# A decoder layer with streamed weights: another order of the mixer's column blocks, and order edges for its two recurrences

## The chip, the cores and the metric

The kernel runs on one core of a Trainium2 chip. A core has a matrix engine (TensorE, PE in the profile), a vector engine (VectorE, DVE), a scalar engine (ScalarE, ACT), GpSimd (POOL), a queue engine (SyncE, SP) and 16 DMA engines. Each engine executes its own list of instructions in order, and semaphores make one engine wait for another. The metric is the device time of one execution in microseconds; less is better.

## The reference

One layer for 256 tokens of width 2048, in float32: a half-step SwiGLU feed-forward part (width 5632), a mixer, and a second half-step feed-forward part, each followed by a layer norm. The mixer puts two kinds of heads side by side: differential attention (8 heads) and RWKV-7 (16 heads of size 64, a recurrence over the tokens).

```python
x = layer_norm(alpha * x + 0.5 * swiglu(x, ffn1_w_gate[l], ffn1_w_up[l], ffn1_w_down[l]),
               ln1_g[l], ln1_b[l])
p = x @ w_in[l]
o_attn = diff_attn_group(p[..., :ATTN_COLS], lambda_q1[l], lambda_k1[l],
                         lambda_q2[l], lambda_k2[l], attn_norm_g[l], lambda_init)
o_rwkv = rwkv7_group(p[..., ATTN_COLS:], rwkv_mu[l], rwkv_w0[l], rwkv_w2[l],
                     rwkv_a0[l], rwkv_a2[l], rwkv_g2[l], rwkv_k_k[l], rwkv_k_a[l],
                     rwkv_r_k[l], rwkv_gn_g[l], rwkv_gn_b[l])
mix = jnp.concatenate([o_attn, o_rwkv], axis=-1) @ w_out[l]
x = layer_norm(alpha * x + mix, ln2_g[l], ln2_b[l])
x = layer_norm(alpha * x + 0.5 * swiglu(x, ffn2_w_gate[l], ffn2_w_up[l], ffn2_w_down[l]),
               ln3_g[l], ln3_b[l])
```

The heart of the RWKV-7 part is a state that every token updates:

```python
sa = jnp.einsum('bhvk,bhk->bhv', state, -kk_t)
state = (state * w_t[:, :, None, :]
         + sa[..., None] * (kk_t * a_t)[:, :, None, :]
         + v_t[..., None] * k_t[:, :, None, :])
return state, jnp.einsum('bhvk,bhk->bhv', state, r_t)
```

## The kernel before

**Streaming.** The 256 tokens are two tiles of 128 (tt = 0 and 1). All weights pass through the core once, in blocks of 256 x 512. `Stream.block` loads such a block as `raw` on SP's DMA queue (3 buffers). ACT rounds it to the matrix engine's 32-bit format as `wh` (L128), and DVE forms the rest as `wl` (L129); each has 7 buffers. PE then makes three products for each 128 rows of a block (L105 to L107: high part by `wh`, high part by `wl`, low part by `wh`), into an accumulator `acc` of 128 x 512. These are the stream matmuls: six for a block and token tile. Tile 1 follows tile 0 four blocks later (`LAG`). The high and low parts of the activations, `xh` and `xl`, are made by ACT (L78) and DVE (L79).

**The mixer** works on four groups: r1 and r2 are the two halves of the RWKV heads, a1 and a2 those of the attention heads. Each group needs three column blocks of `w_in` (512 columns, eight stream steps each): r, k and v for RWKV, q, k and v for attention. A finished accumulator is copied to `tm` (L338) and transposed (L342). The rest of a group's work is written as Python generators: `rwkv_group` prepares the recurrence, runs it and makes r's output (L683 to L727), `rwkv_values` prepares the values, and `attn_heads` computes two heads each. After every stream step `run_bg` advances the generators in turn (`bg`), until the costs that they yield have used up a budget of 1.6 (`BG`). So the text of the program interleaves the generators with the stream, and a scheduler with a timeline then fixes the list of every engine.

**The recurrence of a group** goes over four chunks of 64 tokens. Before it, a triangular inverse is computed by DVE (L577 and L579, 31 pairs), written to memory as `dY` and `dYT`, and read back in another layout as `TT` and `YT` (L583 to L595, all issued by ACT). Products with them on PE follow (L602, L613), then transposes (L623). In each chunk PE's L636 goes to DVE's copy L638, PE's L644 to the copies L645 (DVE) and L646 (ACT), PE's L652 to the new state on DVE (L657 to L662), and L669 and L675 make the output. r1 must be past its chain before r2 may use its buffers (`until`).

**After the recurrence** comes what this document calls r's tail: means on PE (L689), their subtraction on DVE (L690), squares on ACT (L693), sums on PE (L699), logarithm and exponential on ACT, each with its table load (L700, L702), four steps on DVE (L704, L707, L709 and, with PE's L720 and L723, the gate at L724), and the split into `xh` and `xl`.

**w_out** is applied in three parts of its rows, numbered 0 = a1, 1 = a2, 2 = r1, 3 = r2: first (0, 2), then (1,), then (3,). Before each part `ready` drains the groups that it needs. A part adds its product into `y` (L866), and behind the last one the statistics (L868) and `ln_tail` (L176 to L185, and transposes L72) make LN2, on which the second feed-forward part waits.

The column blocks come in the order r1: k r v; a1: v k q; r2: k r v; then a1 is drained; a2: v k q.

## Time and profile before

| | us |
|---|---|
| median of 3 runs (2021.23 to 2022.83) | 2022.36 |
| the profiled execution's own time | 2021.85 |
| span of the profiled execution | 2020.1 |
| mean clock granted to PE | 0.989 of full |

The mixer's recurrences and w_out lie between about 760 and 1290 us of the span; the feed-forward parts are on both sides. A row of the page gives line, engine, operation, tiles (out<-in), count, busy time, the mean of one in ns, and the idle time before with what ended it. A row of a timeline gives start, duration, engine, line, operation and tiles, and in brackets the idle time ahead of it with what ended that. In the rows of windows the numbers in brackets are instruction counts.

### The profile page before, as it was taken

How to read it: one execution, taken by the hardware profiler on the slowest of the kernel's cores; microseconds unless marked ns; L12 is line 12 of the kernel's file. 1: busy time of each engine (PE TensorE's matmuls, PEld its weight loads, DVE VectorE, ACT ScalarE, POOL GpSimd, SP SyncE). 2: the span in 40 equal slices, each digit the busy share in tenths (PEclk: the TensorE clock that was granted, in tenths of full speed). 3: DMA queues.
4: the chain of work that ended last, by engine and by line, in shares of the span. 5: the costliest groups of instructions: out<-in, count | busy, mean ns of one | idle time of the engine just before them, and what ended most of it. 6: DMA issues, size and time to landing. Idle time of an engine off the chain costs nothing. (4 is left out here: it accounts for less than half of the span.)

```text
span 2020.1 us, 24928 instructions
## 1 busy us (share of the span) xinstructions
PE 1976.9 (98%) x9671; PEld 1614.6 (80%) x9671; DVE 1149.0 (57%) x1420; ACT 887.6 (44%) x1100; POOL 33.9 (2%) x68
## 2 busy tenths in 40 slices
PE   9999999999999999999999988999999999999997
PEld 7888888888888878888777777788888888888886
DVE  5555544445554566776677866755554444555455
ACT  5444433344444337645574444444443334444432
POOL 0200000000000000000000000000000000000000
PEclk9999999999999999999999979999999999999999
DMA  7766666667666556556435624666666666766553
GB/s 248 214 188 195 186 190 202 205 192 229 193 187 189 188 171 194 177 160 178 139 86 177 198 84 148 210 198 188 196 185 190 203 204 191 230 193 187 189 188 125
DMA packets 202008, 373.35 MB, mean 185 GB/s; under 512 B 22826, under 2 KB 24944, under 8 KB 201120
## 3 DMA queue, kind: packets, MB, share of 16 engines
q1 hardware_dynamic: 182928, 350.53, 58.0%
q10 hardware_dynamic: 17440, 14.29, 2.4%
q0 software_dynamic: 1520, 6.93, 1.0%
q8 instruction: 76, 1.25, 0.3%
q14 instruction: 44, 0.36, 0.1%
HBM read 364.10 MB, written 7.60 MB: 184 GB/s over the span
## 5 line engine op out<-in xcount | busy, mean ns | idle before, releaser
L129 DVE TENSOR_TENSOR wl<-raw,wh 128x1024 fp32r<-128x1024 f32 (+1 forms) x665 | 808.2, 1216 | 662.4 <-ACT wh L128 661.3
L128 ACT CAST wh<-raw 128x1024 fp32r<-128x1024 f32 (+1 forms) x665 | 695.2, 1046 | 851.9 <-PE acc L107 736.8
L107 PE MATMUL acc<-wh,xl 128*128 128x512 f32 (+1 forms) x1952 | 740.7, 391 | 1.6 <-DVE xl L79 1.6
L106 PE MATMUL acc<-wl,xh 128*128 128x512 f32 (+1 forms) x1952 | 736.7, 392 | 1.0 <-DVE wl L129 1.0
L105 PE MATMUL acc<-wh,xh 128*128 128x512 f32 (+1 forms) x1952 | 725.5, 392 | 9.0 <-ACT xh L78 7.6
L105 PEld LDWEIGHTS acc<-wh,xh 128*128 128x128 f32 x1952 | 367.9, 189 | 88.7 <-ACT xh L78 9.3
L106 PEld LDWEIGHTS acc<-wl,xh 128*128 128x128 f32 x1952 | 368.1, 189 | 77.5 <-issue 2.0
L107 PEld LDWEIGHTS acc<-wh,xl 128*128 128x128 f32 x1952 | 367.8, 188 | 76.3 <-DVE xl L79 2.0
L107 PE MATMUL acc<-wh,hh 128*128 128x512 f32 x704 | 258.0, 395 | 0.0
L106 PE MATMUL acc<-wl,hh 128*128 128x512 f32 x704 | 256.7, 394 | 0.0
L105 PE MATMUL acc<-wh,hh 128*128 128x512 f32 x704 | 256.0, 394 | 0.0
L106 PEld LDWEIGHTS acc<-wl,hh 128*128 128x128 f32 x704 | 132.0, 187 | 31.4
L107 PEld LDWEIGHTS acc<-wh,hh 128*128 128x128 f32 x704 | 132.0, 188 | 31.2
L105 PEld LDWEIGHTS acc<-wh,hh 128*128 128x128 f32 x704 | 132.0, 188 | 30.9
L230 DVE TENSOR_TENSOR hh<-tr,hh 128x512 fp32r<-128x512 f32 x44 | 30.4, 691 | 64.4 <-ACT hh L229 64.4
L229 ACT CAST hh<-tr 128x512 fp32r<-128x512 f32 x44 | 25.8, 586 | 91.7 <-PE tr L221 91.6
L218 DVE SCALAR_TENSOR_TENSOR h<-sg,acc 128x512 f32<-128x512 f32 x44 | 30.3, 688 | 35.6 <-PE acc L107 35.6
L213 ACT ACTIVATE sg<-acc 128x512 f32<-128x512 f32 x44 | 26.4, 600 | 43.8 <-PE acc L107 43.7
L577 DVE TENSOR_TENSOR itmp<-U,Y 64x31 f32<-64x31 f32 (+15 forms) x62 | 20.6, 332 | 11.5 <-DMA U<-dU 10.2
L221 PEld LDWEIGHTS tr<-ident,h 128*128 128x128 f32 x176 | 21.8, 139 | 5.7
L221 PE MATMUL tr<-ident,h 128*128 128x128 f32 x176 | 26.3, 272 | 0.0
L579 DVE TENSOR_TENSOR Y<-Y,itmp 64x31 f32<-64x31 f32 (+15 forms) x62 | 20.6, 332 | 1.4
(247 smaller groups left out, 750.2 us busy)
## 6 DMA issues: line engine op xcount, KB each, us to landing
raw<-in_ffn_w_up_dram SPq DMA_DIRECT2D x176, 512.0 KB, 3.9
raw<-in_ffn_w_down_dram SPq DMA_DIRECT2D x176, 512.0 KB, 4.1
raw<-in_ffn_w_gate_dram SPq DMA_DIRECT2D x175, 512.0 KB, 3.9
raw<-in_w_in_dram SPq DMA_DIRECT2D x96, 512.0 KB, 3.9
raw<-in_w_out_dram SPq DMA_DIRECT2D x32, 512.0 KB, 4.6
rc<-xs ACTq DMA_DIRECT2D x16, 256.0 KB, 4.0
lng<-in_ln_g_dram POOLq DMA_DIRECT2D x3, 1024.0 KB, 7.0
lnb<-in_ln_b_dram POOLq DMA_DIRECT2D x3, 1024.0 KB, 9.3
```

Of the source, the lines that this page charges most:

```text
L105: T.matmul(a, hi, wh[:, j, :w], start=(ki + j == 0), stop=False)
L106: T.matmul(a, hi, wl[:, j, :w], start=False, stop=False)
L107: T.matmul(a, lo, wh[:, j, :w], start=False, stop=(ki + j == last))
L128: SC.copy(out=wh[:, c, :w], in_=raw[:, c, :w])
L129: V.tensor_tensor(out=wl[:, c, :w], in0=raw[:, c, :w], in1=wh[:, c, :w].bitcast(F32), op=ALU.subtract)
L213: SC.activation(out=s, in_=acc, func=AF.Silu)
L218: V.scalar_tensor_tensor(out=h, in0=sg[tt], scalar=0.5, in1=acc, op0=ALU.mult, op1=ALU.mult)
L221: T.transpose(tr[:, i, :], h[:, i * P:(i + 1) * P], ident)
L229: SC.copy(out=hi, in_=tr)
L230: V.tensor_tensor(out=lo, in0=tr, in1=hi.bitcast(F32), op=ALU.subtract)
L577: V.tensor_tensor(out=tv, in0=U[:, 0:j, j:j + 1].to_broadcast([64, j, 32 - j]), in1=Y[:, j:j + 1, j:32].to_broadcast([64, j, 32 - j]), op= ...
L579: V.tensor_tensor(out=Y[:, 0:j, j:32], in0=Y[:, 0:j, j:32], in1=tv, op=ALU.add)
```

## The change

Six things are edited together; the change adds and removes no arithmetic.

- The column blocks come in the order r1: k r v; a1: v, k; r2: k, r; a1: q; r2: v; a2: q; then a1 is drained; a2: v, k. `rwkv_cols` and `attn_cols` take one block per call, and r2's recurrence has its inputs one block sooner.
- w_out's parts come in the order (0, 2), (3,), (1,): r2's is second, a2's last.
- The recurrences' generators go to a list of their own, `hot`. `run_bg` gives it the budget first, and the attention generators another (1.0, `AT`, if `hot` moved).
- `mark` and `behind` add order edges: the last matmul of a recurrence step is marked, and the first matmul of tile 0, two stream steps later, must come behind it in PE's list. The edge orders the list and adds no semaphore.
- The yields' costs change (0.6 to 4.0 ahead of the inverse, 1.0 to 1.6 in it, 0.6 to 6.0 behind its DMAs, 0.6 to 0.8 in the chain).
- Two of the four `y` tiles are put where r2's `TT` and `YT` were.

In the changed kernel the lines are numbered otherwise. L105, L106 and L107 are L118, L121 and L122; L128 is L143; L78 is L79; L338 and L342 are L367 and L371; L583, L584, L591 and L595 are L617, L618, L625 and L629; L602 is L636; L636, L644, L652, L669 and L675 are L671, L680, L689, L707 and L713; L689, L699, L720 and L723 are L727, L737, L758 and L761; L766 is L806, L821 is L861.

```diff
+AT = 1.0
...
+            self.hot = []
             self.bg = []
-            self.credit = 0.0
+            self.credit = [0.0, 0.0]
             self.hooks = {}
             self.step = 0
+            self.marks = []
+
+        def mark(self, inst):
+
+            self.marks.append((self.step, inst.ins))
+
+        def behind(self, inst):
+            while self.marks and self.marks[0][0] + 2 <= self.step:
+                first = self.marks.pop(0)[1]
+                tc.add_manual_dep(inst.ins, first.name, mybir.DependencyInfo(mybir.DependencyClass.NoSync, mybir.DependencyReason.DATA),
+                                  reason="issue order")
...
-                T.matmul(a, hi, wh[:, j, :w], start=(ki + j == 0), stop=False)
+                m = T.matmul(a, hi, wh[:, j, :w], start=(ki + j == 0), stop=False)
+                if tt == 0 and j == 0:
+                    self.behind(m)
...
+        def run_bg(self, budget):
+            moved = False
+            for i, lst in enumerate((self.hot, self.bg)):
+                self.credit[i] = min(self.credit[i], 0.0) + (AT if moved else budget)
+                while self.credit[i] > 0:
+                    cost = self.advance(lst)
+                    if cost is None:
+                        break
+                    moved = True
+                    self.credit[i] -= cost
...
+        def rwkv_state(g, prev=None):
+            st = {"prev": prev, "g": g}
             if prev is not None:
                 prev["next"] = st
             st["gen"] = rwkv_group(g, st)
-            stream.bg.append(st["gen"])
+            stream.hot.append(st["gen"])
+            return st
...
+            i = "rkv".index(name)
+            stream.block(w_in, R0 + i * AW + g * NB, NB, KX, x_lhs, lambda tt, acc: done(tt, acc, i), budget=BG)
...
-            yield 0.6
+            yield 4.0
...
-                    yield 1.0
+                    yield 1.6
...
-            yield 0.6
+            yield 6.0
...
+            order = stream.mark
             for c in range(4):
                 ps = bank("sm", (P, 4, 64))
                 for p in range(4):
                     for e in range(2):
                         k = halves[1 - e] if c == 0 else slice(0, P)
-                        T.matmul(ps[halves[e], p, :], Q[k, p, c, e, 0:64], SV[k, p, c, e, :], start=True, stop=True)
+                        m = T.matmul(ps[halves[e], p, :], Q[k, p, c, e, 0:64], SV[k, p, c, e, :], start=True, stop=True)
                 Rs = mp.tile([P, 4, 64], F32, tag="Rs", name=nm("Rs"))
                 V.tensor_copy(out=Rs, in_=ps)
-                yield 0.6
+                order(m)
+                yield 0.8
...
+                if st["cols"] == 6:
                     st["left"] = 2
                     st["gens"] = [attn_heads(g, st, (i, i + 2)) for i in range(2)]
                     stream.bg.extend(st["gens"])
...
-        r1 = rwkv_cols(0)
-        a1 = attn_cols(0)
-        r2 = rwkv_cols(1, r1)
+        r1, a1, a2 = rwkv_state(0), attn_group(0), attn_group(1)
+        for name in "krv":
+            rwkv_cols(r1, name)
+        attn_cols(a1, "v")
+        attn_cols(a1, "k")
+        r2 = rwkv_state(1, r1)
+        rwkv_cols(r2, "k")
+        rwkv_cols(r2, "r")
+        attn_cols(a1, "q")
+        rwkv_cols(r2, "v")
+        attn_cols(a2, "q")
         stream.drain(gens(a1))
-        a2 = attn_cols(1)
+        attn_cols(a2, "v")
+        attn_cols(a2, "k")
         stream.flush()
...
-        parts = [(0, 2), (1,), (3,)]
+        parts = [(0, 2), (3,), (1,)]
...
                 yt = [hp.tile([P, 2, NB], F32, tag="H3", name=nm("yt")), qq[:, 0].rearrange("p a s -> p (a s)").rearrange("p (t n) -> p t n", t=2),
-                      hp.tile([P, 2, NB], F32, tag=HT["k"], name=nm("yt"))]
-                yj = hp.tile([P, 2, NB], F32, tag="H5", name=nm("yv"))
-                yv = [yj[:, t] for t in range(2)]
-                y = [[yt[n][:, t, :] for n in range(3)] + [yv[t]] for t in range(2)]
+                      hp.tile([P, 2, NB], F32, tag=HT["lw"], name=nm("yt")), hp.tile([P, 2, NB], F32, tag=HT["T1"], name=nm("yt"))]
+                y = [[yt[n][:, t, :] for n in range(4)] for t in range(2)]
```

The first place is PE's list where w_out's first part (0, 2) ends. In the list of the change, `acc_9546` is an accumulator of part (0, 2), the `sm` tiles are r2's tail, `at_9656` and `at_9684` are transposes of a2's last outputs, and `acc_9702` is the first accumulator of the next part, (3,):

```order
L727 MATMUL sm_9459<-BKc,bones 128x256 x2
L727 MATMUL sm_9463<-BKc,bones 128x256 x2
L861 MATMUL at_9656<-ident,ot_9562 128x128 x2
L861 MATMUL at_9684<-ident,ot_9608 128x128
L737 MATMUL sm_9512<-Q,bones 128x256 x2
L737 MATMUL sm_9516<-Q,bones 128x256 x2
L758 MATMUL sm_9592<-gs_5688,Q 128x256 x2
L761 MATMUL sm_9592<-gs_5689,Q 128x256 x2
L861 MATMUL at_9684<-ident,ot_9608 128x128
L758 MATMUL sm_9598<-gs_5688,Q 128x256 x2
L761 MATMUL sm_9598<-gs_5689,Q 128x256 x2
L118 MATMUL acc_9702<-wh_9697,xh_9688 128x512
```

In the list before, the same stretch has r2's recurrence (`sm_8863` to `sm_8943`) and a2's transposes between the end of part (0, 2) and the first matmul of part (1,), which is `acc_9702` there:

```order
L636 MATMUL sm_8863<-SV_8235,Q 64x64 x8
L821 MATMUL at_9576<-ident,ot_9496 128x128 x2
L644 MATMUL sm_8874<-Rs_8872,TT_8541 64x64 x8
L652 MATMUL sm_8885<-SV_8235,BT_8641 64x64
L669 MATMUL sm_8925<-Q,SV_8235 64x64
L652 MATMUL sm_8885<-SV_8235,BT_8641 64x64 x3
L652 MATMUL sm_8885<-SV_8235,BT_8642 64x64 x4
L669 MATMUL sm_8925<-Q,SV_8235 64x64 x7
L675 MATMUL sm_8925<-AR,St_8822 64x64 x8
L821 MATMUL at_9580<-ident,ot_9528 128x128 x2
L636 MATMUL sm_8943<-SV_8235,Q 64x64 x8
L105 MATMUL acc_9702<-wh_9697,xh_9688 128x512
```

r2's tail comes later before, between the stream matmuls of part (1,) (`acc_9822`) and the first of part (3,), `acc_9870`:

```order
L699 MATMUL sm_9031<-Q,bones 128x256 x2
L699 MATMUL sm_9035<-Q,bones 128x256 x2
L720 MATMUL sm_9091<-gs_5688,Q 128x256 x2
L723 MATMUL sm_9091<-gs_5689,Q 128x256 x2
L106 MATMUL acc_9822<-wl_9838,xh_9688 128x512
L107 MATMUL acc_9822<-wh_9837,xl_9689 128x512
L105 MATMUL acc_9822<-wh_9837,xh_9688 128x512
L106 MATMUL acc_9822<-wl_9838,xh_9688 128x512
L107 MATMUL acc_9822<-wh_9837,xl_9689 128x512
L720 MATMUL sm_9167<-gs_5688,Q 128x256 x2
L723 MATMUL sm_9167<-gs_5689,Q 128x256 x2
L105 MATMUL acc_9870<-wh_9865,xh_9856 128x512
```

So r2's recurrence has moved from behind part (0, 2) to among its matmuls, and r2's tail has moved to where the recurrence was, with no stream matmul in it.

The second place is ACT's list around r2's inverse (`dY`). In the list of the change, `tm_8743` and `tm_8781` are copies of a2's k, and `xh_8795` and `xh_8799` are the halves of a1's output that part (0, 2) begins with:

```order
L367 COPY tm_8743<-acc_8562 128x512
L617 DMA dY_8040<-Y_8048 64x1024
L618 DMA dYT_8041<-U_8046 32x1024
L79 CAST xh_8807<-og_7655 128x512
L143 CAST wh_9078<-raw_9077 128x1024
L143 CAST wh_9147<-raw_9146 128x1024
L783 COPY qq<-tr_8443 128x4x128
L625 DMA TT_8703<-dY_8040 32x16x32 x4
L629 DMA YT_8709<-dYT_8041 32x16x32 x2
L783 COPY k_8555<-tr_8745 128x4x128
L367 COPY tm_8781<-acc_8666 128x512
L79 CAST xh_8795<-qq 128x512
```

Before, the attention's work (L789, L803, L806) and the casts of the weights of part (1,) stand around the same DMAs:

```order
L128 CAST wh_9665<-raw_9664 128x1024
L583 DMA dY_8150<-Y_8158 64x1024
L584 DMA dYT_8151<-U_8156 32x1024
L789 COPY pT_9272<-at_9268 128x384
L803 ACTIVATE ot_9278,ss_9279<-at_9274 128x128 x2
L591 DMA TT_8541<-dY_8150 32x16x32 x4
L595 DMA YT_8547<-dYT_8151 32x16x32 x2
L806 ACTIVATE ot_9278,ss_9279<-ot_9278 128x128 x2
L128 CAST wh_9697<-raw_9696 128x1024
L128 CAST wh_9717<-raw_9716 128x1024
L803 ACTIVATE ot_9292,ss_9293<-at_9288 128x128 x2
```

The copies and casts that end a2's column blocks have moved behind the DMA issues (L617 to L629).

The third place is PE's list in r1's recurrence (`SV_6381` is r1's state and values). In the list of the change:

```order
L689 MATMUL sm_7090<-SV_6381,BT_6991 64x64 x4
L707 MATMUL sm_7103<-Q,SV_6381 64x64 x7
L118 MATMUL acc_6940<-wh_7174,xh_5350 128x512
L121 MATMUL acc_6940<-wl_7175,xh_5350 128x512
L122 MATMUL acc_6940<-wh_7174,xl_5351 128x512
L118 MATMUL acc_6940<-wh_7174,xh_5350 128x512
L121 MATMUL acc_6940<-wl_7175,xh_5350 128x512
L122 MATMUL acc_6940<-wh_7174,xl_5351 128x512
L671 MATMUL sm_7151<-SV_6381,Q 64x64 x8
L680 MATMUL sm_7162<-Rs_7160,TT_6825 64x64 x8
```

Before, with `acc_7733` and `acc_7553` as the stream, at the same step:

```order
L636 MATMUL sm_6894<-SV_6381,Q 64x64
L105 MATMUL acc_7733<-wh_7548,xh_5412 128x512
L636 MATMUL sm_6894<-SV_6381,Q 64x64 x7
L793 MATMUL at_7477<-v_6239,pT_7443 128x128
L794 MATMUL at_7477<-v_6239,pT_7443 128x128
L795 MATMUL at_7477<-v_6239,pT_7443 128x128
L106 MATMUL acc_7733<-wl_7549,xh_5412 128x512
L107 MATMUL acc_7733<-wh_7548,xl_5413 128x512
```

Before, 21 stream matmuls follow L636 until L644 comes, and 15 to 24 lie between other steps; now six lie ahead of L671, and L680 follows it at once.

More of the change, by code (lines that the diff above doesn't have):

```diff
@@ L139, in flush, with advance @@
                 self.mm(self.pend.pop(0), 1)
-        def run_bg(self, budget):
-            self.credit = min(self.credit, 0.0) + budget
-            idle = 0
-            while self.bg and self.credit > 0 and idle < len(self.bg):
-                g = self.bg.pop(0)
+        def advance(self, lst):
+            for _ in range(len(lst)):
+                g = lst.pop(0)
                 try:
@@ L422, in done @@
                         st["gen2"] = rwkv_values(g, st)
[L423 to L427 removed]
+                        stream.hot.append(st["gen2"])
+            i = "rkv".index(name)
+            stream.block(w_in, R0 + i * AW + g * NB, NB, KX, x_lhs, lambda tt, acc: done(tt, acc, i), budget=BG)
         def col(i, g, p):
@@ L727, in rwkv_group, with attn_group, attn_cols, done @@
             st["end"] = True
-        def attn_cols(g):
-            st = {"q": qq[:, g],
-                  "k": hp.tile([P, 4, S], F32, tag=HT["k"], name=nm("k"))}
-            vj = hp.tile([P, 2, NB], F32, tag="H5", name=nm("v"))
-            vt = [vj[:, t] for t in range(2)]
-            st["v"] = vt
-            def vdone(tt, acc):
-                SC.copy(out=vt[tt], in_=acc)
-            def qkdone(tt, acc, n):
-                chan_major(acc, tt, [P] * 4, lambda tr: SC.copy(out=st[n][:, :, tt * P:(tt + 1) * P], in_=tr))
-                if n == "q" and tt == 1:
+        def attn_group(g):
+            return {"q": qq[:, g], "g": g, "cols": 0}
+        def attn_cols(st, name):
+            g = st["g"]
+            if name == "k":
+                st["k"] = hp.tile([P, 4, S], F32, tag=HT["k"], name=nm("k"))
+            if name == "v":
+                vj = hp.tile([P, 2, NB], F32, tag="H5", name=nm("v"))
+                st["v"] = [vj[:, t] for t in range(2)]
+            def done(tt, acc):
+                if name == "v":
+                    SC.copy(out=st["v"][tt], in_=acc)
+                else:
+                    chan_major(acc, tt, [P] * 4, lambda tr: SC.copy(out=st[name][:, :, tt * P:(tt + 1) * P], in_=tr))
+                st["cols"] += 1
+                if st["cols"] == 6:
                     st["left"] = 2
```

63 lines of the change are left out of this document (32 added, 31 removed).

## The prediction

> **What bounds the kernel now.** I read the page's head first, then the windows of 10 us, and then the timelines of single engines where a window shows TensorE idle.
>
> ```profile
> span 2020.1 us, 24928 instructions
> PE 1976.9 (98%) x9671; PEld 1614.6 (80%) x9671; DVE 1149.0 (57%) x1420; ACT 887.6 (44%) x1100; POOL 33.9 (2%) x68
> ```
>
> TensorE (PE) is busy for 98% of the span, so time is lost or won only where it waits or is slow. The next fence has steady weight streaming in its first row, then the windows in which that breaks. Columns: window, its length, each engine's busy time, the clock granted to PE, DMA share, GB/s.
>
> ```profile
> 710.00:720.00 10.00, 10.00 (x44) 8.07 (x44) 5.94 (x6) 3.79 (x4) 0.00 (x0) 1.00 0.62 195
> ...
> 1150.00:1160.00 10.00, 7.52 (x94) 6.00 (x92) 3.28 (x10) 4.28 (x16) 1.01 (x1) 0.96 0.65 183
> 1160.00:1170.00 10.00, 7.64 (x106) 5.94 (x108) 6.40 (x20) 5.90 (x12) 1.01 (x1) 0.50 0.49 161
> 1170.00:1180.00 10.00, 7.55 (x92) 6.03 (x92) 7.71 (x22) 3.51 (x13) 0.00 (x0) 0.67 0.11 26
> 1180.00:1190.00 10.00, 8.80 (x104) 7.16 (x101) 7.11 (x27) 4.96 (x24) 1.01 (x1) 0.67 0.19 55
> 1190.00:1200.00 10.00, 8.15 (x100) 6.79 (x101) 6.99 (x22) 4.26 (x10) 1.01 (x1) 1.00 0.01 2
> ...
> 1220.00:1230.00 10.00, 7.80 (x33) 5.59 (x31) 5.75 (x8) 6.32 (x7) 0.00 (x0) 1.00 0.56 176
> 1230.00:1240.00 10.00, 6.30 (x19) 5.04 (x20) 5.62 (x9) 3.09 (x4) 0.54 (x1) 0.66 0.26 105
> ...
> 1260.00:1270.00 10.00, 6.52 (x34) 5.04 (x33) 10.00 (x14) 2.73 (x5) 0.00 (x0) 0.92 0.64 194
> 1270.00:1280.00 10.00, 10.00 (x35) 7.98 (x34) 9.96 (x17) 2.58 (x3) 1.00 (x1) 0.73 0.73 225
> ```
>
> 44 stream matmuls in 10 us make 0.227 us each. Three holes stand out.
>
> **First hole, 1150 to 1200.** The five busy times sum to 39.7 of 50 us, so 10.3 us is idle. The clock column allows at most 9.5 us more (each busy time times its missing clock: 0.3 + 3.8 + 2.5 + 2.9). Small matmuls stretch less than the clock does: comparing each PE record here with the usual pitch of its kind leaves 7.3, so the hole costs 17.6.
>
> **Second hole, 1220 to 1240**, the end of r2 before w_out's last part: 2.2 + 3.7 us idle, and 6.3 x 0.34 = 2.1 of clock, 8.0 together. **Third, 1260 to 1280**, LN2: about 4 us idle and some 3.5 of clock.
>
> In the PE timeline, the first hole is r2's recurrence standing alone, with a2's heads between its steps:
>
> ```profile
> 1157.80 1.54 PE L602 MATMUL sm<-YT,Q 32*32 32x32 f32 x64 [1.71 <-DMA YT<-dYT]
> 1161.83 0.28 PE L613 MATMUL sm<-TT,PT 32*32 32x32 f32 x2 [2.49 <-issue]
> ...
> 1195.86 0.50 PE L105 MATMUL acc<-wh,xh 128*128 128x512 f32 x1 [0.82 <-ACT xh L78]
> ```
>
> Up to 1195.86 no weight is streamed, since w_out part (1,) needs all of a2.
>
> **What the change removes.** In the changed PE list r2's recurrence and a2's heads stand among the streams of w_out part (0,2), as the front's first pieces show, and part (3,) follows, so the first hole goes: -17.6. The second hole changes shape and is counted below as a new one: -8.0. Two more windows:
>
> ```profile
> 1030.00:1080.00 50.00, 47.91 (x241) 36.66 (x240) 43.16 (x60) 33.76 (x46) 0.00 (x0) 1.00 0.40 117
> 900.00:1030.00 130.00, 130.00 (x984) 103.93 (x983) 85.99 (x183) 72.50 (x143) 4.05 (x4) 1.00 0.55 156
> ```
>
> The first is r2's preparation, 2.1 idle. In the changed list a1's q block stands between r2's inputs r and v, and walking those rows with the same durations leaves about 0.8: -1.3. The second holds r1's recurrence, which cost nothing, since it stood among many streams. Removed: **26.9**. The matmuls, casts and DMAs are the same in number; the SP list fetches blocks in the new order, and POOL's list keeps its counts, so I cost these at nothing: the streams that cover the raw loads are as many as before.
>
> **What it adds, place by place.** First **r2's tail**. Every stream matmul that doesn't need r2 comes before it in the PE list; behind the last of them stands a serial chain. Its durations, from the PE, ACT and DVE timelines of the same chain before:
>
> ```profile
> 1212.82 1.46 PE L689 MATMUL sm<-BKc,bones 128*128 128x256 f32 x6
> 1220.72 1.89 PE L699 MATMUL sm<-Q,bones 128*128 128x256 f32 x8
> 1226.67 1.13 PE L723 MATMUL sm<-gs,Q 32*128 32x256 f32 x4
> ```
>
> ```profile
> 1216.16 1.06 ACT L693 ACTIVATE Q<-BKc 128x1024 f32<-128x1024 f32 x1
> ...
> 1222.33 1.28 ACT L700 ACT_TABLE_LOAD   x1
> 1223.63 1.27 ACT L700 ACTIVATE Q<-sm,ge 128x512 f32<-128x512 f32 x2
> 1224.91 1.28 ACT L702 ACT_TABLE_LOAD   x1
> 1226.21 1.06 ACT L702 ACTIVATE Q<-Q 128x1024 f32<-128x1024 f32 x1
> 1233.03 1.14 ACT L78 CAST xh<-og 128x512 fp32r<-128x512 f32 x2 [5.76 <-DVE og L724]
> ```
>
> ```profile
> 1214.75 0.69 DVE L690 SCALAR_TENSOR_TENSOR BKc<-sm,BKc 128x512 f32<-128x512 f32 x1 [0.17 <-PE sm L689]
> 1216.29 1.23 DVE L129 TENSOR_TENSOR wl<-raw,wh 128x1024 fp32r<-128x1024 f32 x1 [0.85 <-ACT wh L128]
> ...
> 1227.30 1.23 DVE L704 TENSOR_TENSOR BKc<-BKc,Q 128x1024 f32<-128x1024 f32 x1 [3.72 <-ACT Q L702]
> ...
> 1229.04 1.38 DVE L707 TENSOR_SCALAR BKc<-BKc,vB 128x256 f32<-128x256 f32 x4
> 1230.45 1.23 DVE L709 TENSOR_TENSOR Q<-BKc,vv 128x1024 f32<-128x1024 f32 x1
> 1231.71 1.29 DVE L724 TENSOR_TENSOR og<-Q,sm 128x512 f32<-128x512 f32 x2
> ```
>
> Half of L689 (0.86), L690 twice (1.4) with a residual L129 queued between (1.2), L693 (1.1), half of L699 (0.95), the two table loads with their activations (4.9), L704 (1.2), L707 (1.4), L709 (1.2), L724 (1.3) and half of L78 (0.6) make 16.1. The changed DVE list queues a2's last scaling and its residuals in this stretch (0.4 + 1.3), and a dozen hand-overs of about 0.05 make it 18.4. PE has some 8.0 of its own in it (L689, L699, L720, L723, a2's last transposes). So it waits 10.5, and 2 of clock follow, the clock loss of the second hole: **+12.5**, bounds 8 and 15. Before, 32 stream matmuls of part (1,) (7.3 us) stood in this chain. That cover is gone.
>
> Next, **ACT behind r2's inverse**. Before, the DMA issues that wait for the inverse's landing held up only a2's heads:
>
> ```profile
> 1153.30 1.95 ACTq L591 DMA_DIRECT2D TT<-dY  x4
> 1155.34 0.98 ACTq L595 DMA_DIRECT2D YT<-dYT  x2
> 1156.37 0.31 ACT L806 ACTIVATE ot<-ot 128x128 f32<-128x128 f32 x1 [5.72 <-DMA TT<-dY]
> ```
>
> ```profile
> dY<-Y ACTq DMA_DIRECT2D x2, 256.0 KB, 4.3
> ...
> L338 ACT COPY tm<-acc 128x512 f32<-128x512 f32 (+1 forms) x22 | 12.5, 567 | 5.1 <-PE acc L107 5.1
> ```
>
> Now a copy of k, the last `tm` copy (L367, was L338) and the casts of a1's output `xh` (L79) are queued behind them on ACT, and the first stream of part (0,2) needs these casts. The `tm` copy ahead of dY can start 3.2 us (14 streams) before PE's last stream; dY then issues at -2.6 and lands at +1.7 by its median of 4.3. The issues of L625 (1.95) and L629 (0.98), the two copies (1.2) and the cast (0.6) end at +6.4. PE has 1.2 of transposes meanwhile: it waits 5, and 2 of clock follow, **+7**, bounds 4 and 9. A 32x32 product that needs YT also precedes that first stream; at 2.5 from L595's issue to L602's start above, it would come at the same time.
>
> Then **the recurrences' steps**. The new order edges pull them forward: six streams (1.36 us) lie between most steps of r1, and none between the two products L671 and L680, where 15 to 24 lay before. The engine work between steps, in the DVE timeline:
>
> ```profile
> 1193.43 0.87 DVE L661 TENSOR_TENSOR SV<-St,PC 64x256 f32<-64x256 f32 x2
> ...
> 1195.08 0.42 DVE L638 COPY Rs<-sm 128x256 f32<-128x256 f32 x1
> ```
>
> Where nothing lies between, 0.42 and its hand-overs show: some 0.6 in each of three steps. Where six streams lie between, a step fits unless a residual (1.23) or cast is ahead of it on DVE or ACT: then 0.5 to 1. I take 5 for r1 (bounds 2 and 9), with seven such meetings. For r2, L602 and L613 waited 1.7 and 2.5 without streams; the copies L649 and L658 now stand behind exponentials on ACT, so I take 3 there and 2.2 for its steps: **+10.2** in all, bounds 4 and 17.
>
> At last **LN2**. The last accumulation of tile 0 now comes 12 streams later, nearer the end, and more residuals stand between its L866 and L185 on DVE, which is at 10.00 and 9.96 in the third hole's windows; the wait grows from about 4 to 7.4: **+3.3**, bounds 0 and 5.
>
> ```profile
> 1267.56 0.63 PE L72 MATMUL sm<-ident,yv 128*128 128x128 f32 x4 [1.74 <-DVE yv L185]
> ```
>
> **Sum.** 12.5 + 7 + 10.2 + 3.3 = 33.0 against 26.9: +6.1. The profiled execution took 2021.85, 0.5 below the median of the runs; 2021.85 + 6.1 = **2028.0**.
>
> One rule of the Trainium skill is weighed here. The third hole's longest single wait is 1.74 us in these rows, and the clock column still falls, to 0.73. The page "TensorE: Matmul & The Clock Gate", section "Part 1: The HAM clock gate", says that half rate comes after at least one idle window of about 3.4 us; by it waits of 1 us in r1's steps cost no clock and the one of 5 us only if a whole window falls into it, so the sum would be up to 2 lower. The row speaks for less idle time being enough.
>
> **Rivals.** *The cover holds*, the one on the other side: the steps meet few residuals, because DVE is at 57% and PE's queue of ready streams absorbs what is late. Then the steps cost 2 in place of 10.2, the ACT stretch 5, LN2 2, the tail 11: 20 against 26.9, 2015. It decides at the step waits: below some 4 us for both recurrences together, the kernel is not slower. For it: the 130 us about r1's recurrence had no idle time before. Against: six streams are 1.36 us, hardly one residual. *Balance*: half the step waits and an ACT stretch without clock loss, 12.5 + 5 + 5 + 3.3 = 25.8, gives 2021. *Dear steps*: each meeting costs a residual and a cast, and waits that follow one another lower the clock through r1's chain, as from 1160 to 1190 before; 10 more, 2038. That the change doesn't do what it says has no chance: the lists show it.
>
> **Chances.** Forecast 0.42 (2023 to 2033), cover holds 0.22 (2011 to 2018), balance 0.20 (2018 to 2023), dear steps 0.16 (2033 to 2043). A measurement can tell 0.2%, or 4 us, from no change: 2018.3 to 2026.4. Of the forecast 0.10 lies below 2026.4, of balance 0.02 below 2018.3, so: faster 0.24, same 0.28, slower 0.48. With 1 in 10 left out on each side the range is 2013 to 2037.
>
> **What would show it.** The windows about r2's recurrence at 10.00 busy and clock 1.00 confirm the -17.6. One hole of 10 us before part (3,), with table loads in it, confirms the tail; a PE wait put down to ACT's `xh` or `tm` as part (0,2) starts confirms the ACT stretch; waits on L680 and L689 in r1 confirm the steps. If these last are under 0.3 us each, the forecast is wrong, and the kernel faster.

## The result, and the profile after

| | before | after |
|---|---|---|
| median, us (lowest to highest, runs) | 2022.13 (2021.23 to 2022.83, 4) | 2035.90 (2032.21 to 2038.79, 4) |
| profiled execution, its span | 2020.1 | 2034.8 |
| mean clock granted to PE | 0.989 | 0.986 |

The ratio is 1.0067, 95% interval 1.005 to 1.0085: the kernel is slower by 0.7%. The forecast was 2028.0, range 2013 to 2037, with slower as the likeliest sign. So the sign and the range held, and the size was too small: 13.8 us measured against 6.1. The range held by 1 us, and the time lies outside the forecast's own band (2023 to 2033) and inside that of the rival "dear steps" (2033 to 2043), which had 0.16. Three executions far slower than the others of their kernels (2195.98 us of the kernel before, 2838.82 of e6_old_blocks, 5080.55 of e10_before_pool) are left out of the times below.

The head of the page after shows the same work as before (3 us more of it on PE, at a lower clock), in a longer span:

```profile
span 2034.8 us, 24936 instructions
PE 1980.0 (97%) x9671; PEld 1616.0 (79%) x9671; DVE 1147.6 (56%) x1420; ACT 888.7 (44%) x1100; POOL 34.2 (2%) x68
```

The windows of 10 us show the new places (columns as before: PE, PEld, DVE, ACT and POOL busy, clock, DMA share, GB/s):

```profile
930.00:940.00 10.00, 9.02 (x104) 7.09 (x98) 6.20 (x6) 5.84 (x7) 0.00 (x0) 1.00 0.65 211
940.00:950.00 10.00, 7.06 (x116) 5.82 (x117) 4.19 (x8) 6.52 (x12) 0.00 (x0) 0.66 0.36 107
950.00:960.00 10.00, 9.38 (x103) 6.90 (x102) 5.94 (x13) 3.93 (x7) 0.00 (x0) 0.82 0.19 55
...
1120.00:1130.00 10.00, 1.18 (x7) 0.53 (x5) 4.03 (x5) 2.90 (x4) 0.00 (x0) 0.71 0.91 242
1130.00:1140.00 10.00, 8.79 (x28) 6.65 (x28) 2.52 (x3) 3.54 (x6) 0.00 (x0) 0.61 0.48 116
1140.00:1150.00 10.00, 9.73 (x194) 7.39 (x194) 7.74 (x19) 7.16 (x19) 0.00 (x0) 1.00 0.11 28
...
1160.00:1170.00 10.00, 9.64 (x131) 7.58 (x131) 9.24 (x30) 3.35 (x14) 2.01 (x2) 1.00 0.66 205
...
1200.00:1210.00 10.00, 7.12 (x61) 5.46 (x60) 8.28 (x27) 5.28 (x17) 2.64 (x3) 0.98 0.74 235
1210.00:1220.00 10.00, 7.22 (x25) 4.97 (x23) 3.51 (x8) 6.03 (x7) 0.00 (x0) 0.84 0.10 35
1220.00:1230.00 10.00, 6.24 (x22) 5.02 (x22) 5.86 (x9) 3.24 (x4) 0.59 (x1) 0.67 0.29 107
...
1270.00:1280.00 10.00, 4.36 (x20) 3.27 (x18) 9.88 (x16) 4.20 (x4) 1.00 (x1) 0.89 0.71 213
1280.00:1290.00 10.00, 7.96 (x30) 6.62 (x31) 9.97 (x17) 2.35 (x4) 0.56 (x1) 0.60 0.69 210
```

The long hole of before, 1150 to 1200, is gone: r2's recurrence now runs from 1140 to 1205, and 1160 to 1170, at 9.64, is the least busy of the windows up to 1200. In its place stand r1's recurrence (930 to 960), the start of w_out (1120 to 1140), r2's tail (1200 to 1230) and LN2 (1270 to 1290).

To compare kernels whose lists differ, I cut the stream at numbered stream matmuls. In each stretch I sum what every PE record took beyond the usual pitch of its kind, so waits and slow clock both count. Between the two kernels these sums differ by 13.5 in the mixer and by 1.7 before it; the spans differ by 14.7. What counts as usual is a choice: with the median by shape or by line, from start to start or from end to end, single stretches move by up to 2 us (r2's preparation and the hole most), and the sum of all differences lies between 11 and 21. So the table says where the time went; that it adds up to the span so closely is partly chance.

| PE time beyond its usual pitch, us | r1's recurrence (3890 to 3960) | r2's preparation (3960 to 4400) | w_out's start (4400 to 4440) | r2's steps (4440 to 4584) | hole and r2's tail (4584 to 4700) | LN2 (4780 to 4830) |
|---|---|---|---|---|---|---|
| before | -0.4 | 6.5 | 0.0 | 1.1 | 28.0 | 7.0 |
| after | 10.0 | 3.6 | 14.0 | 3.4 | 13.7 | 11.0 |

Two of these stretches are larger than forecast, and both show ACT's list behind the read-back of an inverse. In ACT's timeline after, at r1's inverse:

```profile
918.31 1.05 ACT L143 CAST wh<-raw 128x1024 fp32r<-128x1024 f32 x1 [1.71 <-PE acc L122]
920.50 1.95 ACTq L625 DMA_DIRECT2D TT<-dY  x4
922.49 5.38 ACTq L629 DMA_DIRECT2D YT<-dYT  x2
927.91 0.59 ACT L446 COPY praw<-tr 128x512 f32<-128x512 f32 x1 [8.55 <-DMA YT<-dYT]
```

and at r2's, with PE's timeline of the same time below it:

```profile
1118.42 0.48 ACTq L617 DMA_DIRECT2D dY<-Y  x1
...
1123.22 0.31 ACTq L625 DMA_DIRECT2D TT<-dY  x1
...
1123.56 2.94 ACTq L625 DMA_DIRECT2D TT<-dY  x3
1126.54 3.50 ACTq L629 DMA_DIRECT2D YT<-dYT  x2
1130.08 0.59 ACT L783 COPY k<-tr 128x512 f32<-128x512 f32 x1 [5.97 <-DMA raw<-in_w_out_dram]
...
1130.57 0.59 ACT L367 COPY tm<-acc 128x512 f32<-128x512 f32 x1
1131.04 1.15 ACT L79 CAST xh<-qq 128x512 fp32r<-128x512 f32 x2
```

```profile
1121.83 0.63 PE L371 MATMUL tr<-ident,tm 128*128 128x128 f32 x4 [1.28 <-DVE qq L862]
1131.21 1.11 PE L371 MATMUL tr<-ident,tm 128*128 128x128 f32 x4 [8.76 <-ACT tm L367]
```

PE's timeline of r1's recurrence after shows what reached PE there:

```profile
937.59 0.22 PE L647 MATMUL sm<-TT,PT 32*32 32x32 f32 x2 [0.98 <-issue]
...
942.40 1.33 PE L647 MATMUL sm<-TT,PT 32*32 32x32 f32 x62 [2.37 <-ACT PT L638]
...
949.50 1.12 PE L680 MATMUL sm<-Rs,TT 64*64 64x64 f32 x16 [0.57 <-ACT df L377]
...
957.48 0.68 PE L680 MATMUL sm<-Rs,TT 64*64 64x64 f32 x16 [0.62 <-DVE Rs L673]
...
964.21 0.68 PE L680 MATMUL sm<-Rs,TT 64*64 64x64 f32 x16 [0.52 <-DVE Rs L673]
```

L629's two issues held ACT's queue for 5.38 and 3.50 us, where the row before the change at r2 had 0.98. ACT's copies and weight casts stand still behind the landing of dY and these issues: 8.55 us at r1, and PE waits 8.76 at r2 for the `tm` copy. The releaser printed for the k copy (a raw load) is the latest semaphore the profile saw; the issue rows directly ahead of it are what the queue was doing.

At r2's tail, ACT's two table loads are followed by PE's wait for the halves of r2's output:

```profile
1211.53 1.28 ACT L738 ACT_TABLE_LOAD   x1 [2.15 <-PE sm L737]
...
1214.11 1.28 ACT L740 ACT_TABLE_LOAD   x1
```

```profile
1223.77 0.79 PE L118 MATMUL acc<-wh,xh 128*128 128x512 f32 x1 [6.54 <-ACT xh L79]
```

and at LN2 PE waits once, for the result of tile 0:

```profile
1281.36 1.11 PE L73 MATMUL at<-ident,yt 128*128 128x128 f32 x4 [7.01 <-DVE yt L214]
```

### The profile page after: what moved, and what is told of

Same layout as the page of the kernel before. It is cut to its first block, busy times and chain, and to the rows that moved or that the text cites. A ratio compares the mean times of both kernels' runs of the same rounds, so it can differ in the third digit from the quotient of the medians.

```text
span 2034.8 us, 24936 instructions
## 1 busy us (share of the span) xinstructions
PE 1980.0 (97%) x9671; PEld 1616.0 (79%) x9671; DVE 1147.6 (56%) x1420; ACT 888.7 (44%) x1100; POOL 34.2 (2%) x68
## 4 chain that ended last, share of the span: by engine, by line
PE 93%; DVE 3%; DMA 2%; ACT 1%; issue 1%; ACTq 0%; DVEq 0%; SPq 0%
PE acc L118 29%; PE acc L121 29%; PE acc L122 29%; PE tr L250 1%; DMA raw<-in_w_out_dram 1%; DVE wl L144 1%; PE sm L588 1%; ACT wh L143 1%; PE at L806 1%; DMA raw<-in_w_in_dram 1%; DVE y L213 0%; DMA raw<-in_ffn_w_gate_dram 0%; PE tr L371 0%; PE tr L73 0%; DVE y L214 0%
## 5 line engine op out<-in xcount | busy, mean ns | idle before, releaser
L143 ACT CAST wh<-raw 128x1024 fp32r<-128x1024 f32 (+1 forms) x665 | 695.0, 1046 | 842.2 <-PE acc L122 735.6
L122 PE MATMUL acc<-wh,xl 128*128 128x512 f32 (+1 forms) x1952 | 740.8, 391 | 0.5 <-DVE xl L80 0.5
L121 PE MATMUL acc<-wl,xh 128*128 128x512 f32 (+1 forms) x1952 | 737.8, 393 | 0.0
L118 PE MATMUL acc<-wh,xh 128*128 128x512 f32 (+1 forms) x1952 | 728.5, 393 | 9.4 <-ACT xh L79 6.5
L118 PEld LDWEIGHTS acc<-wh,xh 128*128 128x128 f32 x1952 | 368.5, 189 | 88.7 <-ACT xh L79 8.7
L121 PEld LDWEIGHTS acc<-wl,xh 128*128 128x128 f32 x1952 | 368.8, 189 | 75.2 <-DVE wl L144 1.0
L122 PEld LDWEIGHTS acc<-wh,xl 128*128 128x128 f32 x1952 | 368.6, 189 | 74.5 <-DVE xl L80 0.7
L122 PE MATMUL acc<-wh,hh 128*128 128x512 f32 x704 | 258.0, 395 | 0.0
L121 PE MATMUL acc<-wl,hh 128*128 128x512 f32 x704 | 256.7, 394 | 0.0
L118 PE MATMUL acc<-wh,hh 128*128 128x512 f32 x704 | 256.0, 394 | 0.0
L121 PEld LDWEIGHTS acc<-wl,hh 128*128 128x128 f32 x704 | 132.0, 187 | 31.3
L122 PEld LDWEIGHTS acc<-wh,hh 128*128 128x128 f32 x704 | 132.0, 188 | 31.2
L118 PEld LDWEIGHTS acc<-wh,hh 128*128 128x128 f32 x704 | 132.0, 188 | 30.9
L247 DVE SCALAR_TENSOR_TENSOR h<-sg,acc 128x512 f32<-128x512 f32 x44 | 30.3, 688 | 34.7 <-PE acc L122 34.7
L371 PE MATMUL tr<-ident,tm 128*128 128x128 f32 (+1 forms) x86 | 14.0, 282 | 10.0 <-ACT tm L367 8.8
```

The costliest lines, as they stand in the source:

```text
L118: m = T.matmul(a, hi, wh[:, j, :w], start=(ki + j == 0), stop=False)
L121: T.matmul(a, hi, wl[:, j, :w], start=False, stop=False)
L122: T.matmul(a, lo, wh[:, j, :w], start=False, stop=(ki + j == last))
L143: SC.copy(out=wh[:, c, :w], in_=raw[:, c, :w])
L247: V.scalar_tensor_tensor(out=h, in0=sg[tt], scalar=0.5, in1=acc, op0=ALU.mult, op1=ALU.mult)
```

## The experiments

Twelve kernels; each was compared with the kernel before in shared runs, in which that one's median lay between 2022.70 and 2023.41. Ratios are to the kernel before; the changed kernel has 1.0067.

**e1_pool_dma**: the read-back DMAs are issued by GpSimd.

```diff
-                nc.scalar.dma_start(out=TT[rr, :, cc], in_=dY[uu].rearrange("u s t -> s u t"))
+                nc.gpsimd.dma_start(out=TT[rr, :, cc], in_=dY[uu].rearrange("u s t -> s u t"))
...
-                nc.scalar.dma_start(out=YT[64 * e:64 * e + 32], in_=dYT[16 * e:16 * e + 16].rearrange("u s t -> s u t"))
+                nc.gpsimd.dma_start(out=YT[64 * e:64 * e + 32], in_=dYT[16 * e:16 * e + 16].rearrange("u s t -> s u t"))
```

> The changed kernel with only the read-back DMAs of the inverse (TT and YT, L625 and L629) issued by GpSimd instead of ACT. Theory (ACT's blocked list): in the changed kernel ACT's issues of these DMAs lasted 3.3 and 3.5 us behind the wait for dY, and the tm copy, the k copy and the casts of a1's output stood behind them, so PE lost 14 us where part (0, 2) begins; that shrinks to about 3, and the time falls from 2035.9 to some 2024. Rival (the data themselves are late): PE's product that needs YT waits as long, and the time stays within 3 us of 2035.9.

Measured: 2028.96, ratio 1.0032 (1.0018 to 1.0046), halfway between theory and rival. The gain of 6.9 came from a place neither had named: r1's recurrence fell from 10.0 to 2.6. At w_out's start 14.0 fell to 7.7, but r2's steps rose from 3.4 to 11.3, so the two together went from 17.4 to 19.0. PE's timeline of this kernel shows the wait at w_out's start replaced by short waits at r2's first products:

```profile
1130.36 0.96 PE L636 MATMUL sm<-YT,Q 32*32 32x32 f32 x28
1132.17 0.28 PE L647 MATMUL sm<-TT,PT 32*32 32x32 f32 x2 [0.86 <-issue]
...
1134.74 1.91 PE L647 MATMUL sm<-TT,PT 32*32 32x32 f32 x62 [1.24 <-ACT PT L638]
```

and its window of 1130 to 1140 has PE at 7.77 and the clock at 0.50:

```profile
1130.00:1140.00 10.00, 7.77 (x126) 6.25 (x125) 6.13 (x18) 8.44 (x24) 0.00 (x0) 0.50 0.01 2
```

How ACT's stall reaches PE at r1, some 10 us later, can be followed in the traces. While ACT makes no casts, the three `raw` buffers stay full and the weight loads stop. The window of 926 to 931 shows it, first in the changed kernel, then in this one:

```profile
926.00:931.00 5.00, 4.91 (x80) 3.72 (x79) 1.52 (x2) 3.09 (x5) 0.00 (x0) 1.00 0.23 31
926.00:931.00 5.00, 5.00 (x46) 3.87 (x46) 1.22 (x1) 1.52 (x2) 0.00 (x0) 1.00 1.02 269
```

In the changed kernel ACT's casts at 934.47 and 937.01 then wait 2.64 and 1.49 us for their loads, and the copy of `PT` (L638), for which PE waits 2.37 us, stands behind them and ends at 942.4. Here a cast waits too (3.46 us at 929.94), but its load comes some 5 us sooner: the copy of `PT` ends at 937.1, and none of PE's waits between 935 and 966 is longer than 0.62 us.

**e9_r1_pool**: the same for r1's recurrence alone.

```diff
-                nc.scalar.dma_start(out=TT[rr, :, cc], in_=dY[uu].rearrange("u s t -> s u t"))
+                (nc.gpsimd if g == 0 else nc.scalar).dma_start(out=TT[rr, :, cc], in_=dY[uu].rearrange("u s t -> s u t"))
...
-                nc.scalar.dma_start(out=YT[64 * e:64 * e + 32], in_=dYT[16 * e:16 * e + 16].rearrange("u s t -> s u t"))
+                (nc.gpsimd if g == 0 else nc.scalar).dma_start(out=YT[64 * e:64 * e + 32], in_=dYT[16 * e:16 * e + 16].rearrange("u s t -> s u t"))
```

> The changed kernel with the read-back DMAs on GpSimd for r1 only; r2's stay on ACT. Theory (ACT's issues held up r1, while r2's stretch is bound by the round trip of the inverse itself): PE's loss in r1's recurrence falls from 9 to 2 us as in e1_pool_dma, the 16 us between stream matmuls 4400 and 4500 stay, and the time is that of e1_pool_dma, 2028 to 2030. Rival (r2's issues on ACT cost something of their own): 2031 to 2036 here, since only a part of e1_pool_dma's gain is r1's.

Measured: 2029.98, ratio 1.0034 (1.002 to 1.0047), as the theory said. r1's recurrence lost 2.5 here, w_out's start 14.2, r2's steps about 7. So the 7 us of e1_pool_dma are r1's, and moving r2's issues off ACT moves r2's wait: these last two stretches together lose 17.4 in the changed kernel, 19.0 in e1_pool_dma and some 21 here.

**e10_before_pool**: the kernel before, with its L591 and L595 on GpSimd.

```diff
-                nc.scalar.dma_start(out=TT[rr, :, cc], in_=dY[uu].rearrange("u s t -> s u t"))
+                nc.gpsimd.dma_start(out=TT[rr, :, cc], in_=dY[uu].rearrange("u s t -> s u t"))
...
-                nc.scalar.dma_start(out=YT[64 * e:64 * e + 32], in_=dYT[16 * e:16 * e + 16].rearrange("u s t -> s u t"))
+                nc.gpsimd.dma_start(out=YT[64 * e:64 * e + 32], in_=dYT[16 * e:16 * e + 16].rearrange("u s t -> s u t"))
```

> The kernel before with its read-back DMAs (L591, L595) on GpSimd, nothing else. Theory (ACT's issues cost time only where the edges or w_out's first part wait for ACT): r1's recurrence lost nothing before and the hole of r2 is a chain, so the time stays within 4 us of 2022.5. Rival (GpSimd's issue is a gain of its own, and e8_pool_parts owes its lead to that alone): 2015 to 2018.

Measured: 2026.52, ratio 1.0022 (1.0012 to 1.0031): slower by 4 us, at the edge of what the theory allowed, and against the rival. r1's recurrence stayed at -1.1, where the kernel before had -0.4. The hole grew from 28.0 to 36.7, since r2's two reads of YT landed after 6.3 and 5.8 us (2.4 and 2.3 before) and PE has nothing else to do there. The row of PE's timeline to set against 1.71 before:

```profile
1162.55 2.07 PE L602 MATMUL sm<-YT,Q 32*32 32x32 f32 x64 [8.62 <-DMA YT<-dYT]
```

The late landing need not be GpSimd's. In the kernel before, no cast of ACT stands between 1147.73 and 1156.97, weight loads pause, and the window of 1155 to 1158 shows 108 GB/s. Here ACT is free and casts at 1150.31 and 1153.74, and the same window shows 229. In e4_all_three, where GpSimd reads back at a time of few loads (79 GB/s from 1150 to 1155), r2's two reads of YT landed after 2.4 us, as from ACT before. So freeing ACT let weight loads run into the read-back; no run here holds the loads fixed and changes the engine alone.

The same ACT stall stands in the kernel before: 2.18 and 3.00 us of issue at r1, as ACT's timeline before shows. It cost PE nothing, because 15 to 24 stream matmuls stood between r1's steps.

```profile
918.69 2.18 ACTq L591 DMA_DIRECT2D TT<-dY  x4
920.92 3.00 ACTq L595 DMA_DIRECT2D YT<-dYT  x2
923.96 0.59 ACT L741 COPY qq<-tr 128x512 f32<-128x512 f32 x1 [6.15 <-issue]
```

**e2_r2_edges** and **e7_r1_edges**: order edges for one recurrence only.

```diff
-            order = stream.mark
+            order = stream.mark if g == 1 else (lambda m: None)
```

> The changed kernel with order edges for r2's recurrence only. Theory (edges pull r1's steps together): about 21 streams again lie between r1's steps, the 10.5 us that PE loses between 925 and 975 us go, and the time is about 2025. Rival (pacing): the waits of r1 come from the yields and the hot list, which stay; the time stays at 2034 to 2037. Second rival: r1 ends later, r2 starts later, and half of the 10.5 comes back at r2: 2030.

Measured: 2046.81, ratio 1.0124 (1.0106 to 1.0142). All three expectations fell. The 10 us in r1 did go (0.3 there), but r2's steps went from 3.4 to 33.6. In ACT's rows dY of r2 is issued at 1118.4 after the change and at 1146.2 here: r2's preparation uses r1's buffers, so it can't run ahead of r1's chain, and PE's last L713 of r1 starts at 984.0 after the change and at 1014.6 here. r1's edges cost at r1 and buy r2's early start. PE's windows of this kernel show the price:

```profile
1120.00:1130.00 10.00, 5.22 (x28) 3.24 (x26) 9.25 (x27) 2.99 (x12) 0.00 (x0) 0.94 0.52 164
1130.00:1140.00 10.00, 4.80 (x18) 3.62 (x18) 9.52 (x40) 4.66 (x24) 1.09 (x1) 0.50 0.00 0
1140.00:1150.00 10.00, 6.87 (x20) 4.08 (x20) 8.95 (x31) 0.03 (x1) 1.09 (x1) 0.50 0.18 39
```

DVE stands at 9 there, with r2's inverse and a2's softmax in one queue, and PE's list has only products that wait for them.

```diff
-            order = stream.mark
+            order = stream.mark if g == 0 else (lambda m: None)
```

> The changed kernel with order edges for r1's recurrence only. Theory (r2's edges are what keeps its steps among the streams of part (0, 2)): two chunks of r2 now stand behind the last of these streams, with 6 to 10 us of new idle time there, while the 10 us in r1 stay: 2042 to 2046. Rival: r2's edges cost what they gain, 2034 to 2038.

Measured: 2035.12, ratio 1.0062 (1.0043 to 1.0082), as the rival said. Without r2's edges its steps lose 1.1 in place of 3.4, and the tail 16.2 in place of 13.7: no difference that can be told.

**e3_parts_back**: w_out's parts in the old order.

```diff
-        parts = [(0, 2), (3,), (1,)]
+        parts = [(0, 2), (1,), (3,)]
```

> The changed kernel with w_out's parts in the old order (0, 2), (1,), (3,). Theory (r2's tail lost its cover): part (1,) can start when a2's last transposes are done, some 10 us before the end of r2's tail, which it then hides; PE's loss between 1200 and 1235 us falls from 13 to about 4, and the time is about 2027. Rival (a2 ends as late as r2): part (1,) starts hardly earlier, 2033 to 2036.

Measured: 2028.26, ratio 1.0027 (1.0016 to 1.0038), near the theory's time in the median of runs from 2023.22 to 2033.17. The profiled run was the slowest of these; in it hole and tail fell from 13.7 to 9.1, which is half of what was expected. Part (1,) begins when a2's last transposes are done, before r2's tail ends.

**e5_old_pacing**: the yields of before.

```diff
-            yield 4.0
+            yield 0.6
...
-                    yield 1.6
+                    yield 1.0
...
-            yield 6.0
+            yield 0.6
...
-                yield 0.8
+                yield 0.6
```

> The changed kernel with the yields' costs of before (0.6, 1.0, 0.6, 0.6). Theory (the pacing puts r2's inverse too late): with smaller costs the inverse runs ahead, r2's first product with YT stands behind stream matmul 4278 instead of 4416 and its tail ahead of the end of part (0, 2), so that the 14 us where part (0, 2) begins and the 13 us of the tail go; 10 us of new waits stand at 4278 where several steps follow without streams between. Time 2018 to 2024. Rival (the inverse's DVE work crowds out the residuals): new waits of 15 to 25 us earlier in the mixer, time 2030 to 2040.

Measured: 2053.12, ratio 1.0154 (1.0139 to 1.017). The theory fell, and the rival's reason too. ACT's rows give r1's dY at 916.2 here and at 916.5 after the change: the yields hardly move the inverse of r1. They move where the product that needs it stands in PE's list: here behind stream matmul 3744, after the change behind 3874, so that 130 stream matmuls which could have run stand behind a wait. w_out's start did lose nothing (0.4), as the theory had it, but the stretch of the tail kept 11.2, and the clock stood at 0.50 in the windows from 910 to 930, behind this wait. PE's row:

```profile
923.85 2.06 PE L636 MATMUL sm<-YT,Q 32*32 32x32 f32 x64 [18.98 <-DMA YT<-dYT]
```

**e6_old_blocks**: the column blocks in the old order.

```diff
-        r2 = rwkv_state(1, r1)
-        rwkv_cols(r2, "k")
-        rwkv_cols(r2, "r")
         attn_cols(a1, "q")
+        r2 = rwkv_state(1, r1)
+        rwkv_cols(r2, "k")
+        rwkv_cols(r2, "r")
         rwkv_cols(r2, "v")
-        attn_cols(a2, "q")
         stream.drain(gens(a1))
         attn_cols(a2, "v")
         attn_cols(a2, "k")
+        attn_cols(a2, "q")
```

> The changed kernel with the column blocks in the old order (r1: k r v; a1: v k q; r2: k r v; a2: v k q), edges, pacing and parts as changed. Theory (one block sooner matters): r2's inputs k and r come one block later, its inverse is ready later, and PE waits 10 us more behind stream matmul 4440, where a1's and r2's products stand; 2046. Rival (edges and pacing alone set r2): the same as the changed kernel, 2033 to 2038.

Measured: 2040.81, ratio 1.0091 (1.007 to 1.0111), between the two. r2's dY is issued at 1137.0 in place of 1118.4, and r2's steps lose 22.9 in place of 3.4; but w_out's start loses nothing (14.0 in the changed kernel), since no copy of it stands behind the read-back any more. The block order is worth about 5 us.

**e4_all_three** (GpSimd, r2's edges alone, old parts, each edit as above):

> All three edits of this series in one kernel. Theory (three separate places): the gains add, 2035.9 less 11, 10.5 and 9, about 2005. Rival (they share one cause, or one takes the other's place): 2015 to 2022, no better than the kernel before.

Measured: 2030.01, ratio 1.004 (1.0024 to 1.0056). The gains don't add: without r1's edges r2's steps lose 34.7 here too. The sum of single guesses was wrong in the one that e2_r2_edges had wrong.

**e8_pool_parts** (GpSimd and old parts, both recurrences with their edges):

> The changed kernel with the read-back DMAs on GpSimd and w_out's parts in the old order, both recurrences with their edges. Theory (the two places are apart): the 7 us that GpSimd's issue won, and 7 us at r2's tail, where part (1,) runs while the tail ends; about 2022. Rival (part (1,) waits as late as part (3,) did, since a2's heads now end later): 2027 to 2029.

Measured: 2018.76, ratio 0.9977 (0.9967 to 0.9986), better than either kernel and than the theory's 2022. Hole and tail lose 4.8, r1's recurrence 2.6, r2's steps still 11.2. Against e1_pool_dma, from which only the order of the parts differs, the tail's stretch falls by 9 and the time by 10 us.

**e11_pacing_9**: e8_pool_parts with r2's first product put 48 stream matmuls later in PE's list, r1's 4 later, and what follows them later too.

```diff
-            yield 6.0
+            yield 9.0
```

> e8_pool_parts with the yield behind the inverse's DMAs at 9.0 in place of 6.0. In its PE list r2's first product with YT stands behind stream matmul 4488 in place of 4440, a2's last transposes ahead of the end of part (0, 2), and r2's tail among the matmuls of part (1,). Theory (the steps of r2 then find their data landed): the 9 us between 4440 and 4500 fall to about 5 and the 5 us at 4584 go, 2009 to 2014. Rival (r2 ends too late for part (3,)): 5 to 10 us of idle time before part (3,), 2018 to 2024.

Measured: 2009.71, ratio 0.9931 (0.9914 to 0.9947), the best of all, 26 us below the changed kernel. The theory's time holds, and its terms in part: the tail is hidden (1.1), w_out's start is free (0.4), LN2 is back at 7.1, but r2's steps lose 13.5, not 5. Its windows from r2's steps to the tail:

```profile
1130.00:1140.00 10.00, 7.73 (x101) 5.76 (x100) 8.68 (x17) 6.90 (x15) 1.27 (x2) 0.94 0.78 213
1140.00:1150.00 10.00, 9.44 (x131) 8.22 (x131) 3.42 (x14) 6.12 (x22) 0.70 (x1) 0.50 0.14 50
...
1180.00:1190.00 10.00, 10.00 (x102) 8.12 (x101) 7.85 (x24) 5.65 (x13) 1.91 (x2) 1.00 0.34 106
1190.00:1200.00 10.00, 9.27 (x81) 7.35 (x80) 5.99 (x11) 3.19 (x6) 0.62 (x1) 1.00 0.68 211
1200.00:1210.00 10.00, 10.00 (x46) 8.39 (x45) 6.92 (x9) 4.25 (x5) 0.00 (x0) 1.00 0.52 175
```

**e12_pacing_9_act**: e11_pacing_9 with the read-back issued by ACT again (`nc.gpsimd` back to `nc.scalar` in both lines of e1's diff).

> e11_pacing_9 with the read-back DMAs on ACT again, so the changed kernel with w_out's parts in the old order and the yield at 9.0. Theory (ACT's issues cost r1 some 7 us, whatever the pacing): r1's recurrence loses 9 to 11 us again and the time is 2016 to 2020. Rival (with that pacing nothing on PE is close behind ACT's issues): within 3 us of e11_pacing_9, 2007 to 2013.

Measured: 2015.95, ratio 0.9958 (0.9941 to 0.9975): the theory's time, 6 us above e11_pacing_9, but not its place. r1's recurrence loses 6.0 (3.5 with GpSimd), not 9 to 11, and LN2 11.1 (7.1). So with this pacing r1 loses less to ACT's issues than in the changed kernel; through which of the moved products was not tried. Why LN2 differs by 4 was not tried.

## Why the prediction was right in sign and short in size

- **The first hole goes, and r2's tail takes its place.** Right. Forecast -17.6 - 8.0 + 12.5 = -13.1; measured 13.7 - 28.0 = -14.3. The tail has the forecast form: table loads in it, no stream, and a slow clock behind it. PE waits 9.4 us in it (0.58, 2.30 and 6.54), for 10.5 forecast. e3_parts_back confirms its cause, and e8_pool_parts against e1_pool_dma does so more clearly: with the part of a2 second, the loss falls by 5 and by 9.
- **LN2.** Forecast +3.3, measured +4.0, with the forecast cause: DVE puts tile 0's statistics together (L205, before L176) 0.3 us ahead of the end of PE's last stream, 6.0 before, and PE waits 7.01 in one piece in place of 0.68, 1.74 and 1.07. But the order of the parts alone doesn't set it: with the old order e3_parts_back and e12_pacing_9_act lose 11 us there, e11_pacing_9 7.
- **r2's start** (-1.3) and **r2's steps** (+5.2): measured -2.9 and +2.3. Both were judged a little too dear.
- **ACT behind r2's inverse: the mechanism was right and the term mis-sized**, +7 forecast, +14.0 measured. The step that failed took the issues of L625 and L629 from their rows before, 1.95 and 0.98 us. After the change they last 3.3 and 3.5 us, in a window whose DMA share is 0.91. ACT's other rows before, at r1, already had 2.18 and 3.00, and the prediction took the shorter pair. PE's waits there are 10.0 us (1.28 and 8.76) for 5 forecast: 3.9 of the difference are these issues, and 1.0 is dY, which was issued half a microsecond later than forecast and took longer to land. The other 4.0 are the slow clock, forecast at 2. e1_pool_dma and e9_r1_pool add that this wait isn't bought off by issuing from GpSimd: the products of r2 that follow wait for the same round trip, and the two stretches together lose as much (19.0 against 17.4).
- **r1's steps: the size was off and the reason was the wrong one**, +5 forecast for short waits between the edges, +10.4 measured. The waits between L671 and L680 are as forecast (three, 0.5 to 0.6 us in PE's rows). But with the read-back moved off ACT r1 loses only 2.6: so 7 of the 10 us are ACT's stall behind r1's DMAs and the slow clock behind it (5.1 of the 10 are waits), which the prediction named for r2 alone. The edges matter because they take away the streams that had hidden that stall before: in e2_r2_edges, with a stall of 6.99 us on ACT and no edges at r1, r1 loses 0.3.
- **What r1's edges are worth** was not in the prediction at all. It counted them as cost; e2_r2_edges shows that without them r2's inverse comes 28 us later and the kernel is 11 us slower.

The terms that were too small add 12.4 (7.0 and 5.4). With the three that were too dear or missed a gain (-2.9, -1.6, -1.2), LN2's 0.7 and 1.7 ahead of the mixer, the forecast of 6.1 becomes 15.2, against a span that grew by 14.7. That errors of 5.7 the other way hid nearly half of the 12.4, and kept the time inside the range, is luck.

Of the rivals, "dear steps" came nearest in time (2038) and named r1's chain, though with residuals and casts as the reason. "The cover holds" fell at the point it had named: the two recurrences lose 12.7 us more than before, not under 4.

The clock went as the row of before suggested. In r1's stretch after, PE's longest single wait is 2.37 us, and the windows still show the clock at 0.66 and 0.82. The Trainium skill, "TensorE: Matmul & The Clock Gate", section "Part 1: The HAM clock gate", asks for an idle window of some 3.4 us; read strictly, that rule would have kept the clock. The rows show that a shorter wait with small products around it was enough; why, no run here tried.

## What to carry to other kernels

An instruction that waits for a DMA's landing holds up everything behind it in its engine's list. Before moving one, list what stands behind it on that engine, and take the longest issue row in the trace, not the shortest. An engine that is set free also starts things: ask which loads will then run beside the transfer that it issued. A dependence that looks like pure cost, such as an order edge, may be what lets the next stage start early, so price it by the date at which the next stage's first input is ready. In kernels of in-order lists, put the waiting product where its data have landed: one yield's cost, from 6.0 to 9.0, was worth 9 us here.
